# Low parts of weights by adding DMAs, sums of squares on TensorE, and shared copies in the first mixer of a two-block transformer

## The chip, the cores and the metric

The kernel runs as one program on one core of a Trainium2 chip. The core has five engines that each run their own list of instructions in order and meet by semaphores: PE (TensorE, matrix products), DVE (VectorE), ACT (ScalarE), POOL (GpSimd) and SP (SyncE, which here only issues DMAs). PSUM holds the results of TensorE; everything else that an engine works on lies in SBUF. The metric is the device time of one execution in microseconds. Before the change the median of 3 runs is 2953.4 us (2951.94 to 2958.28).

## The reference

Two transformer blocks on 256 positions of width 2048, in float32. The change lies in the mixer of the first block:

```python
hn = _rmsnorm(h, attn_norm_w[l])
proj = hn @ w_in[l]                         # 2048 x 1856
u, c_q, c_kv, k_pe = jnp.split(proj, split_at, axis=-1)
y_ssm = _s5_group(u, ...)                   # 64 groups, 64 states, scan over 256 positions,
                                            # gelu, times sigmoid(y @ w_glu + b_glu)
y_mla = _mla_group(c_q, c_kv, k_pe, ...)    # norm, up projections, rotation, 8 causal heads
y = jnp.concatenate([_rmsnorm(y_ssm, ssm_out_norm_w[l]),
                     _rmsnorm(y_mla, mla_out_norm_w[l])], axis=-1)
h = h + y @ w_out[l]
h = h + _conv_ffn(_rmsnorm(h, ffn_norm_w[l]), ...)
```

The second block (a chunked state-space mixer and an RWKV-7 mixer, then a gated feed-forward part) and the first block's feed-forward part are computed by code that does not change.

## The kernel before

**Weights in two parts.** Float32 products are made on TensorE from numbers of reduced precision (type fp32r). A weight block of eight 128 x 128 tiles is a *piece* (`piece`, L322 to L336): SP loads it into `raw` (128 x 1024, 512 KB, 4 buffers), ACT rounds it into the high part `wh` (L329, 3 buffers), and the low part `wl` = raw − wh (L335, 3 buffers) is made by DVE or POOL. A counter chooses: every piece adds `self.pl` to `self.pc`, and when that reaches 1 the piece goes to POOL. `self.pl` is taken from the table `PB`, stage by stage: 0.625 gives POOL five pieces of eight, 1.0 all of them, 0.0 none. The activations are split the same way (`split`, L407 and L408). In the first mixer (`self.one` true) `mm` then issues three matmuls per tile, high weight by low activation, high by high, low by high (L349 to L351), 24 per piece, in this order tile by tile.

**The stages of the first mixer** (`block1_mix`), in the order of the program:

1. The input is loaded and split; the squares of its 16 tiles are summed for the norm (`Sums`), whose result `r1` scales the results of the first product when they leave PSUM (L381, into `u` or `c`).
2. The product with `w_in`, 15 column tiles of two pieces: tiles 0 to 2 with `PB[0]`, 3 to 7 with `PB[1]`, and 12, 13, 14, 8, 9, 10, 11 with `PB[2]`. Between them lie the four batches of the state-space layer (`ssm_batch`: expansions by `ssm_ef`, L616, L617 and L620, on DVE; small products, L359 and L659; evictions to `X` on ACT, L669), two scans over batches 0, 1 and 2, 3 (`ssm_scan`, L701 to L722, all on DVE), and the expansions of the output side (`ssm_f`, the same lines on POOL).
3. The small norms and projections of the attention (`small_norm`, `mla_proj`, ten pieces with `PB[3]`), the attention itself, and the activation of the state-space layer (`ssm_g`), which gathers its result by sixteen copies per batch on ACT (L755).
4. The product with `w_out`: 16 pieces of the attention half, 8 pieces of the `w_glu` product between them (`glu_tile`), then 16 pieces of the state-space half; `PB[4]` and `PB[5]`.

**Sums of squares.** `Sums` squares each tile on ACT (L209), POOL adds the squares up (L213), and TensorE sums the running total and the last square over partitions, with a column of ones (`mmc`, L359, two matmuls of 64 columns each time).

**What sets the order.** A scheduler orders every engine's list when the program is built, by dependences and its estimates; the order of the source is its starting point, not its result. A piece's copy has to wait until the matmuls of three pieces earlier have let go of their buffer. SP loads ahead as far as the four `raw` buffers allow; a `raw` buffer comes free when its low part is made.

**Other helpers.** `rope_tables` (L473 to L477 with its callees) makes sine and cosine of the rotation, from a DMA of the positions; `bcast` and `rsqrt` (L419 to L434) turn a sum into a scale for all partitions, by way of POOL and TensorE.

Of the kernel before, what the change touches and what calls it, by code (L numbers as in the profile page):

```python
# [10 lines left out]
F32 = mybir.dt.float32  # L11
F32R = mybir.dt.float32r
I32 = mybir.dt.int32
AF = mybir.ActivationFunctionType
ALU = mybir.AluOpType
# [3 lines left out]
P = 128  # L19
# [169 lines left out]


X0 = [(0, 2, 0, 4), (2, 2, 4, 4), (4, 4, 8, 8), (8, 4, 0, 0), (12, 4, 0, 0)]
PB = [0.0, 0.625, 1.0, 1.0, 0.625, 0.625]
EV = [(1, 2), (1, 4, 5, 8), 4, 1]
TK = [18, 17, (44, 19), (34, 12), 6, 10, 56, 7, (7, 7, 7), 14, 16]

# [1 line left out]
class Sums:  # L197


    def __init__(self, k, n, c=0, tag="qa", out=None, last=True):  # L200
        self.k, self.n, self.c, self.i, self.out, self.last = k, n, c, 0, out, last
        self.acc = k.t(tag=tag)

    def add(self, src, scale=1.0, on_act=True):
        k, nc = self.k, self.k.nc
        self.i += 1
        sq = self.acc if self.i == 1 else k.t(tag="sq")
        if on_act:
            nc.scalar.activation(sq, src, AF.Square, scale=scale)  # L209
        else:  # L210
            nc.vector.tensor_tensor(sq, src, src, op=ALU.mult)
        if 1 < self.i < self.n:
            nc.gpsimd.tensor_tensor(self.acc, self.acc, sq, op=ALU.add)  # L213
        if self.i == self.n:
            first = self.out is None
            self.out = k.ssq_start() if first else self.out
            for q in (self.acc, sq):
                for b in range(2):
                    c = self.c + b
                    k.mmc(self.out[:, c:c + 1], q[:, b * P:b * P + P], k.ones[:, 0:1],  # L220
                          first and b == 0 and q is self.acc, self.last and b == 1 and q is sq)


class K:
    def __init__(self, ctx, tc, A, dbg=None):
        self.tc, self.nc, self.A, self.ctx = tc, tc.nc, A, ctx
        self.dbg = dbg or {}
        E = ctx.enter_context
        self.cst = E(tc.tile_pool(name="cst", bufs=1))
        self.raw = E(tc.tile_pool(name="raw", bufs=4))  # L230
        self.wh = E(tc.tile_pool(name="wh", bufs=3))
        self.wl = E(tc.tile_pool(name="wl", bufs=3))
        self.tmp = E(tc.tile_pool(name="tmp", bufs=3))
        self.sm = E(tc.tile_pool(name="sm", bufs=2))
        self.big = E(tc.tile_pool(name="big", bufs=1))
        dr = E(tc.tile_pool(name="dr", bufs=1, space=bass.MemoryType.DRAM))
        self.nd = [dr.tile([32, 32, 32], F32, name=f"n_d{i}") for i in range(8)]
        self.nd2 = [dr.tile([32, 32, 32], F32, name=f"m_d{i}") for i in range(8)]
        self.csd = dr.tile([32, T], F32, name="cs_d")
        self.ysd, self.yrd, self.hd, self.hd2 = [dr.tile([P, 16, T], F32, name=n)  # L240
                                                 for n in ("ys_d", "yr_d", "h_d", "i_d")]
        self.pn = E(tc.tile_pool(name="pn", bufs=1, space=PSUM))
        self.pp = E(tc.tile_pool(name="pp", bufs=1, space=PSUM))
        self.banks = list(range(7))
        self.bgs = []
        self.fibs = []
        self._n = 0
        self.pc = 0
        self.pl = 0
        self.hp = 400  # L250
        self.one = False

    def nm(self, s="t"):
# [69 lines left out]
    def piece(self, ap, nb):  # L323
        nc = self.nc
        r = self.raw.tile([P, KP * P], F32, name=self.nm("raw"), tag="raw")[:, :nb * P]
        h = self.wh.tile([P, KP * P], F32R, name=self.nm("wh"), tag="wh")[:, :nb * P]
        l = self.wl.tile([P, KP * P], F32R, name=self.nm("wl"), tag="wl")[:, :nb * P]
        nc.sync.dma_start(r, ap)
        nc.scalar.activation(h, r, AF.Copy)  # L329
        self.pc += self.pl  # L330
        eng = nc.vector
        if self.pc >= 1:
            eng = nc.gpsimd
            self.pc -= 1
        eng.tensor_tensor(l, r, h.bitcast(F32), op=ALU.subtract)  # L335
        return h, l  # L336

# [402 lines left out]
    def ssm_g(self, b):  # L740

        nc = self.nc
        V, S = nc.vector, nc.scalar
        Z = self.Z[b]
        g = self.ph.tile([P, 8, 64], F32, name=self.nm("sg"), tag="sg", bufs=1)
        S.activation(g, Z, AF.Square)
        V.tensor_scalar(g, g, 0.044715, 1.0, ALU.mult, ALU.add)
        V.tensor_tensor(g, g, Z, op=ALU.mult)
        S.activation(g, g, AF.Tanh, scale=math.sqrt(2.0 / math.pi))
        V.scalar_tensor_tensor(g, g, 1.0, Z, ALU.add, ALU.mult)  # L750
        for q in range(4):
            for s in range(4):
                dst = self.u[32 * q:32 * q + 32, 2 * b:2 * b + 2].rearrange("p j (c s) -> p j s c", s=4)[:, :, s]
                sl = slice(32 * s, 32 * s + 32)
                S.activation(dst, g[sl, 2 * q:2 * q + 2], AF.Copy)  # L755
        for j in range(2 * b, 2 * b + 2):
            self.split(self.gl[:, j], self.u[:, j])

# [34 lines left out]
    def small_norm(self, x, nt, dst, gname):  # L793

        nc = self.nc
        q = Sums(self, nt)
        for i in range(nt):
            q.add(x[:, i])
        r = self.rsqrt(q.out, nt * P)
        rb = self.t(tag="ev")  # L800
        self.bcast(r, rb)
        for i in range(nt):
            y = self.t(tag="ev")
            nc.vector.tensor_tensor(y, x[:, i], rb, op=ALU.mult)
            self.split(dst[:, i], y, self.v(gname, i))
# [92 lines left out]

    def block1_mix(self):
        nc, A = self.nc, self.A  # L900
        self.one = True
        xx = self.xx_new()
        self.hh = [self.b([8, T], f"hh{i}") for i in range(2)]
        pc0 = []
        for k, kn, w0, wn in X0:
# [3 lines left out]
            for i in range(k, k + kn):  # L909
                last = self.split(xx(i), self.h(i), self.v("attn_norm_w", i))  # L910
        self.setup2()
        pst = Sums(self, 16)
        with self.tc.issue_after(last.ins):
            for k in range(16):
                pst.add(self.h(k))
# [2 lines left out]
        self.ssm_pre()  # L918
        self.bglu = self.ssm.tile([P, 8], F32, name="bglu")
        nc.vector.tensor_scalar(self.bglu, self.vs("ssm_b_glu"), 0.5, None, ALU.mult)  # L920
        self.rope_tables()
        self.kpe = [self.mla.tile([P, T], F32, name=f"kpe{i}") for i in range(2)]
        for i in range(2):
            nc.vector.memset(self.kpe[i], 0.0)
# [3 lines left out]
        for n in range(8):  # L928
            self.pl = PB[0] if n < 3 else PB[1]
            p = self.gemm(A["w_in"][n], 16, xx, pcs=pc0 if n == 0 else None)  # L930
# [5 lines left out]
        c = self.ssm.tile([P, 8, T], F32, name="c", tag="u")  # L936
        self.pl = PB[2]
        for i, n in enumerate((12, 13, 14, 8, 9, 10, 11)):
# [7 lines left out]
                    self.ssm_f(k)  # L946
            if i == 2:
                self.ssm_scan(2, 2)
            if i in (3, 4):
                self.ssm_y(i - 3)  # L950
            if i == 5:
# [45 lines left out]
        pst = Sums(self, 16)  # L997
        for n in range(16):
# [5 lines left out]
            nc.vector.tensor_tensor(self.h(n), self.h(n), t, op=ALU.add)  # L1004
            self.split(xx(n), self.h(n), self.v("ffn_norm_w", n))
            pst.add(self.h(n))
        self.one = False
        if "h1" in self.dbg:
            for i in range(2):
                nc.gpsimd.dma_start(self.dbg["h1"][:, 8 * i:8 * i + 8], self.hh[i])  # L1010
# [828 lines left out]
```

## Time and profile before

| | |
|---|---|
| median of 3 runs | 2953.4 us (2951.94 to 2958.28) |
| profiled execution | 2956.56 us, of which the span from first to last instruction is 2954.8 us |
| busy in the span: PE, DVE, ACT, POOL | 2808.0 us (95%), 1974.3 (67%), 1523.8 (52%), 889.5 (30%) |
| mean DMA rate | 166 GB/s |
| first mixer | from 0 to about 450 us |

Times in the profile are microseconds from the start of the span unless marked ns. An instruction is named by its line, its engine, its operation and its tiles, `out<-in`, with the buffers' numbers left out. A window's row has the stretch, its length, then for PE, PEld (the loading of weights into TensorE), DVE, ACT and POOL the busy time and in brackets the count of instructions; then the clock granted to TensorE as a part of full speed, the share of time in which the 16 DMA engines were busy, and the GB/s that they moved. A wait's row has the instruction that waited, the one it waited for, and then the microseconds in all, the number of times, and the longest. A row of a group has the count, the busy time, the mean duration, and the idle time of the engine just before.

### The profile page before, as it was taken

The numbers are of one execution on the slowest core, as the hardware profiler recorded it, in microseconds if no ns is written. First come the engines' busy times: TensorE is split into PE (matmuls) and PEld (weight loads), VectorE is DVE, ScalarE is ACT, GpSimd is POOL, SyncE is SP. The second block draws the span as 40 slices with busy tenths as digits, with TensorE's granted clock in tenths as the row PEclk, the third lists the DMA queues.
The fourth block names the chain that finished last, engine by engine and source line by source line (L and its number), as shares of the span: only waits on it lengthen the run. The fifth ranks groups of instructions, "written<-read, shape, count | busy, mean of one in ns | idle before, by whom it ended". The sixth has DMA issues, their size and how long they took to land.

```text
span 2954.8 us, 54809 instructions
## 1 busy us (share of the span) xinstructions
PE 2808.0 (95%) x21648; PEld 2530.9 (86%) x21648; DVE 1974.3 (67%) x3385; ACT 1523.8 (52%) x2569; POOL 889.5 (30%) x716
## 2 busy tenths in 40 slices
PE   6767899999999999999999999998999999999998
PEld 6766898888888888999998999988988888888887
DVE  9995578886378876887767767774674544354544
ACT  6527655555455555555545555553554444444454
POOL 6565573333333334100110111000023333333333
PEclk8887999999999999999999999999999999999999
DMA  4222255556655556555554444445755656655564
GB/s 165 82 81 78 88 175 180 183 190 181 187 188 187 186 181 199 196 184 185 183 165 127 134 124 132 125 144 152 249 183 185 191 181 186 189 189 185 187 183 151
DMA packets 178978, 490.37 MB, mean 166 GB/s; under 512 B 44416, under 2 KB 61600, under 8 KB 178208
## 3 DMA queue, kind: packets, MB, share of 16 engines
q1 hardware_dynamic: 176992, 483.13, 52.1%
q8 instruction: 170, 2.79, 0.4%
q0 software_dynamic: 288, 2.10, 0.2%
q10 hardware_dynamic: 1440, 1.63, 0.2%
q14 instruction: 88, 0.72, 0.1%
HBM read 474.17 MB, written 12.62 MB: 165 GB/s over the span
## 4 chain that ended last, share of the span: by engine, by line
PE 78%; DMA 2%; DVE 2%; ACT 1%; SPq 1%; issue 1%; POOL 0%; POOLq 0%; DVEq 0%; ACTq 0%
PE acc L353 35%; PE acc L354 18%; PE acc L349 7%; PE acc L350 6%; PE acc L351 6%; PE pc L1351 1%; PE pm L1468 1%; DVE wl L335 1%; PE pm L1630 1%; PE pc L1356 1%; PE py L1259 0%; DMA n_d<-hh 0%; PE pm L1351 0%; SPq L1532 0%; ACT wh L329 0%
## 5 line engine op out<-in xcount | busy, mean ns | idle before, releaser
L329 ACT ACTIVATE wh<-raw 128x1024 fp32r<-128x1024 f32 (+2 forms) x873 | 908.3, 1042 | 999.5 <-PE acc L353 459.8
L335 DVE TENSOR_TENSOR wl<-raw,wh 128x1024 fp32r<-128x1024 f32 (+2 forms) x682 | 861.1, 1263 | 602.7 <-ACT wh L329 595.8
L353 PE MATMUL acc<-xx,wh 128*128 128x512 f32 x2176 | 770.9, 396 | 0.5 <-ACT wh L329 0.5
L354 PE MATMUL acc<-xx,wl 128*128 128x256 f32 x2176 | 614.7, 283 | 0.8 <-DVE wl L335 0.8
L335 POOL TENSOR_TENSOR wl<-raw,wh 128x1024 fp32r<-128x1024 f32 (+1 forms) x191 | 454.6, 2381 | 532.4 <-ACT wh L329 517.0
L353 PEld LDWEIGHTS acc<-xx,wh 128*128 128x128 f32 x2176 | 409.9, 188 | 99.1 <-ACT wh L329 0.7
L354 PEld LDWEIGHTS acc<-xx,wl 128*128 128x128 f32 x2176 | 409.7, 188 | 1.5 <-DVE wl L335 1.4
L353 PE MATMUL acc<-B,wh 128*128 128x512 f32 x960 | 344.7, 396 | 0.0
L353 PE MATMUL acc<-X,wh 128*128 128x512 f32 x960 | 344.4, 396 | 0.0
L349 PE MATMUL acc<-B,wh 128*128 128x256 f32 x960 | 287.5, 300 | 5.6 <-ACT xx L379 3.2
L350 PE MATMUL acc<-B,wh 128*128 128x256 f32 x960 | 272.5, 284 | 0.0
L351 PE MATMUL acc<-B,wl 128*128 128x256 f32 x960 | 272.2, 284 | 0.0
L354 PE MATMUL acc<-B,wl 128*128 128x256 f32 x960 | 271.2, 282 | 1.0 <-POOL wl L335 1.0
L354 PE MATMUL acc<-X,wl 128*128 128x256 f32 x960 | 270.8, 282 | 0.0
L349 PE MATMUL acc<-X,wh 128*128 128x256 f32 x832 | 251.2, 302 | 5.8 <-ACT wh L329 4.5
L351 PE MATMUL acc<-X,wl 128*128 128x256 f32 x832 | 235.5, 283 | 0.8 <-DVE wl L335 0.8
L350 PE MATMUL acc<-X,wh 128*128 128x256 f32 x832 | 235.1, 283 | 0.0
L353 PEld LDWEIGHTS acc<-X,wh 128*128 128x128 f32 x960 | 180.5, 188 | 43.6
L353 PEld LDWEIGHTS acc<-B,wh 128*128 128x128 f32 x960 | 180.5, 188 | 43.4
L213 POOL TENSOR_TENSOR qa<-qa,sq 128x256 f32<-128x256 f32 x86 | 90.0, 1046 | 346.5 <-ACT sq L209 250.1
L349 PEld LDWEIGHTS acc<-B,wh 128*128 128x128 f32 x960 | 184.2, 192 | 11.3 <-ACT xx L379 3.4
L350 PEld LDWEIGHTS acc<-B,wh 128*128 128x128 f32 x960 | 184.3, 192 | 0.6
(497 smaller groups left out, 5255.9 us busy)
## 6 DMA issues: line engine op xcount, KB each, us to landing
raw<-in_w_up_dram SPq DMA_DIRECT2D x264, 512.0 KB, 3.6
raw<-in_w_in_dram SPq DMA_DIRECT2D x213, 512.0 KB, 3.6
raw<-in_w_down_dram SPq DMA_DIRECT2D x128, 448.0 KB, 3.9
raw<-in_w_out_dram SPq DMA_DIRECT2D x96, 512.0 KB, 4.3
raw<-in_w_gate_dram SPq DMA_DIRECT2D x88, 512.0 KB, 4.2
raw<-in_w_down_dram SPq DMA_DIRECT2D x64, 512.0 KB, 4.1
raw<-in_w_glu_dram SPq DMA_DIRECT2D x8, 512.0 KB, 3.5
cb<-cs_d SPq DMA_DIRECT2D x16, 256.0 KB, 3.9
```

The costliest lines, as they stand in the source:

```text
L213: nc.gpsimd.tensor_tensor(self.acc, self.acc, sq, op=ALU.add)
L329: nc.scalar.activation(h, r, AF.Copy)
L335: eng.tensor_tensor(l, r, h.bitcast(F32), op=ALU.subtract)
L349: nc.tensor.matmul(p[:, :T], h, x[:, 1], start=first, stop=False)
L350: nc.tensor.matmul(p[:, :T], h, x[:, 0], start=False, stop=False)
L351: nc.tensor.matmul(p[:, :T], l, x[:, 0], start=False, stop=last)
L353: nc.tensor.matmul(p, h, x.rearrange("p a b -> p (a b)"), start=first, stop=False)
L354: nc.tensor.matmul(p[:, T:], l, x[:, 0], start=False, stop=last)
L1351: self.nc.tensor.matmul(out[hs], lhsT[hs], rhs[hs], start=start, stop=stop)
L1356: self.nc.tensor.matmul(out[64 * h:64 * h + 64], lhsT(h), rhs(h), start=start, stop=stop)
L1468: nc.tensor.matmul(p[:, P * c:P * c + P], z[:, c], AR[:, c].rearrange("p a t -> p (a t)"), start=True, stop=True)
L1630: nc.tensor.matmul(pg[:, T * i:T * i + T], lw[:, 256 * i + P * k:256 * i + P * k + P], self.tgd[:, k], start=k == 0, stop=k == 1)
```

## The change

1. `PB[3]` becomes 0.0: the ten pieces of `mla_proj` give their low parts to DVE.
2. A flag `self.acc` is true in all of `block1_mix`. Where the counter says POOL and the flag is set, the low part is made in another way: a second ACT instruction writes raw times −1 into `wl`, rounded like `wh`, and POOL issues a DMA that adds `raw` to what stands there (`accum_op=ALU.add`). This meets 6 pieces of tiles 3 to 7, 14 of the later tiles, and 25 of the 40 pieces of stage 4.
3. `Sums` gets a way `pe=True`: TensorE adds up every square itself, four matmuls a square, and POOL adds nothing. It is used in the first norm and in `small_norm`.
4. The call of `rope_tables` moves behind the second scan.
5. `ssm_g` gives every second of its copies to DVE: 8 of 16 per batch, 32 in all.

```diff
-PB = [0.0, 0.625, 1.0, 1.0, 0.625, 0.625]
+PB = [0.0, 0.625, 1.0, 0.0, 0.625, 0.625]
...
-    def __init__(self, k, n, c=0, tag="qa", out=None, last=True):
-        self.k, self.n, self.c, self.i, self.out, self.last = k, n, c, 0, out, last
-        self.acc = k.t(tag=tag)
+    def __init__(self, k, n, c=0, tag="qa", out=None, last=True, pe=False):
+        self.k, self.n, self.c, self.i, self.out, self.last, self.pe = k, n, c, 0, out, last, pe
+        self.acc = None if pe else k.t(tag=tag)
...
+        if self.pe:
+            if self.i == 1:
+                self.out = k.ssq_start()
+            for b in range(2):
+                k.mmc(self.out[:, b:b + 1], sq[:, b * P:b * P + P], k.ones[:, 0:1],
+                      self.i == 1 and b == 0, self.i == self.n and b == 1)
+            return
...
         if self.pc >= 1:
+            self.pc -= 1
+            if self.acc:
+                nc.scalar.activation(l, r, AF.Copy, scale=-1.0)
+                nc.gpsimd.dma_start(l.bitcast(F32), r, accum_op=ALU.add)
+                return h, l
             eng = nc.gpsimd
-            self.pc -= 1
...
-                S.activation(dst, g[sl, 2 * q:2 * q + 2], AF.Copy)
+                if s % 2:
+                    V.tensor_copy(dst, g[sl, 2 * q:2 * q + 2])
+                else:
+                    S.activation(dst, g[sl, 2 * q:2 * q + 2], AF.Copy)
...
-        q = Sums(self, nt)
+        q = Sums(self, nt, pe=True)
...
-        self.one = True
+        self.one = self.acc = True
...
-        pst = Sums(self, 16)
+        pst = Sums(self, 16, pe=True)
...
-        self.rope_tables()
...
                 self.ssm_scan(2, 2)
+                self.rope_tables()
...
-        self.one = False
+        self.one = self.acc = False
```

The new lines stand at 335 to 348 in the changed file: L337 is the copy, L343 the negation, L344 the DMA and L347 the subtraction.

How the built lists change. First POOL in tiles 12 to 11, beside the two scans. `wl` is a low part; `ef`, `FA` and `FB` are the expansions of `ssm_f`; `rb` is a product of the rotation. Before:

```order
L616 TENSOR_TENSOR ef_2213<-PA,scq_2210 128x256
L335 TENSOR_TENSOR wl_1378<-raw_1376,wh_1377 128x1024
L335 TENSOR_TENSOR wl_1512<-raw_1510,wh_1511 128x1024
L617 TENSOR_TENSOR ef_2214<-PA,scq_2210 128x256
L335 TENSOR_TENSOR wl_1542<-raw_1540,wh_1541 128x1024
L335 TENSOR_TENSOR wl_1823<-raw_1821,wh_1822 128x1024
L335 TENSOR_TENSOR wl_1853<-raw_1851,wh_1852 128x1024
```

After:

```order
L344 DMA wl_1276<-raw_1274 128x1024
L344 DMA wl_1402<-raw_1400 128x1024
L344 DMA wl_1537<-raw_1535 128x1024
L344 DMA wl_1568<-raw_1566 128x1024
L344 DMA wl_1850<-raw_1848 128x1024
L344 DMA wl_1881<-raw_1879 128x1024
L344 DMA wl_1969<-raw_1967 128x1024
```

The subtractions are gone from the list and DMA issues stand in their places; the expansions that stood among them stand ahead of or behind this run.

Second DVE, at the tables of the rotation, before the first tile of `w_in`. `ev` holds the angle and what becomes of it, `k` and `xc` belong to the preparation of the state-space layer. Before:

```order
L778 TENSOR_SCALAR ev_460<-ev_460,vec 128x256
L506 SCALAR_TENSOR_TENSOR xc_252<-xc_252,xb_251 128x32
L473 TENSOR_SCALAR ev_465<-ev_460 128x256
L509 SCALAR_TENSOR_TENSOR k_249<-xc_252,xi_267 128x32
L474 TENSOR_SCALAR ev_465<-ev_465 128x256
```

After:

```order
L793 TENSOR_SCALAR ev_2164<-ev_2164,vec 128x256
L518 SCALAR_TENSOR_TENSOR xc_294<-xc_294,xb_293 128x32
L485 TENSOR_SCALAR ev_2169<-ev_2164 128x256
L521 SCALAR_TENSOR_TENSOR k_291<-xc_294,xi_309 128x32
L486 TENSOR_SCALAR ev_2169<-ev_2169 128x256
```

The numbers of the buffers show that the call was made later; the instructions stand in the same rows of the list, between the same neighbours.

Third ACT, in stage 4, among the tiles of `w_glu` (`ys` and `sq` are the split and the square of such a tile, `acc` is a PSUM tile). Before:

```order
L329 ACTIVATE wh_3816<-raw_3815 128x1024
L329 ACTIVATE wh_3857<-raw_3856 128x1024
L379 ACTIVATE ev_3770<-acc_3739 128x256
L765 ACTIVATE ev_3770<-ev_3770,bglu 128x256
L407 ACTIVATE ys_3408<-ev_3773,vec 128x256
L209 ACTIVATE sq_3777<-ev_3773 128x256
```

After:

```order
L337 ACTIVATE wh_3967<-raw_3966 128x1024
L343 ACTIVATE wl_3968<-raw_3966 128x1024
L337 ACTIVATE wh_4009<-raw_4008 128x1024
L391 ACTIVATE ev_3920<-acc_3889 128x256
L337 ACTIVATE wh_4043<-raw_4042 128x1024
L343 ACTIVATE wl_4044<-raw_4042 128x1024
L780 ACTIVATE ev_3920<-ev_3920,bglu 128x256
```

A negation (L343) follows the copy of each piece whose low part is made by a DMA, and the evictions and activations stand behind it.

Last DVE, at the end of the second scan (L731 to L734), where `mla_proj`'s low parts now appear:

```order
L731 TENSOR_TENSOR sc_2156<-AK,X_497 128x196
L347 TENSOR_TENSOR wl_2698<-raw_2696,wh_2697 128x1024
L732 TENSOR_TENSOR sc_2157<-AK,X_497 128x196
L733 TENSOR_TENSOR X_497<-X_497,sc_2156 128x4x7x7
L819 TENSOR_TENSOR ev_2522<-c,ev_2517 128x256
L819 TENSOR_TENSOR ev_2526<-c,ev_2517 128x256
L734 TENSOR_TENSOR X_497<-X_497,sc_2157 128x4x7x7
```

In the list before the change no low part stands among these rows (L719 to L722 there).

## Rows read from the trace of the kernel before

**Rows 1.** Windows, by stage: engines' busy us (instructions), granted clock, DMA share, GB/s.

```profile
0.00:36.00 36.00, 22.41 (x146) 20.74 (x147) 31.24 (x86) 24.77 (x50) 23.90 (x31) 0.91 0.70 242
36.00:123.00 87.00, 69.31 (x837) 65.58 (x835) 80.50 (x159) 48.97 (x99) 51.30 (x44) 0.86 0.31 98
123.00:164.00 41.00, 30.20 (x386) 28.94 (x386) 40.12 (x92) 21.99 (x40) 12.66 (x5) 0.88 0.20 65
164.00:228.00 64.00, 35.63 (x301) 32.53 (x301) 63.14 (x106) 11.15 (x17) 40.04 (x29) 0.72 0.23 77
228.00:332.00 104.00, 77.68 (x530) 69.29 (x529) 49.52 (x96) 75.94 (x185) 49.08 (x44) 0.82 0.16 51
332.00:450.00 118.00, 112.94 (x941) 110.80 (x941) 85.99 (x95) 62.55 (x102) 87.20 (x61) 0.99 0.53 174
```

**Rows 2.** Waits of DVE, 36 to 228 us: total us, times, longest.

```profile
DVE B L620 <- PE sp L659: 3.8, 2, 2.8
```

**Rows 3.** Waits of PE, 36 to 228 us, the two longest.

```profile
PE sp L359 <- ACT X L669: 8.9, 1, 8.9
PE sp L359 <- DVE B L620: 8.8, 4, 3.2
```

**Rows 4.** Timeline of DVE, 133 to 141 us: start us, us, instruction.

```profile
133.20 0.65 DVE L704 TENSOR_TENSOR X<-X,sc 128x256 f32<-128x256 f32 x1
133.88 2.60 DVE L701 TENSOR_TENSOR sc<-A,X 128x256 f32<-128x256 f32 x1
136.40 2.87 DVE L702 TENSOR_TENSOR sc<-A,X 128x256 f32<-128x256 f32 x1
```

**Rows 5.** Timeline of POOL, 133 to 141 us.

```profile
133.40 5.32 POOL L335 TENSOR_TENSOR wl<-raw,wh 128x1024 fp32r<-128x1024 f32 x2 [15.30 <-ACT wh L329]
```

**Rows 6.** Groups by line of POOL, 36 to 226 us.

```profile
L335 POOL TENSOR_TENSOR wl<-raw,wh 128x1024 fp32r<-128x1024 f32 x23 | 59.5, 2590 | 56.9 <-ACT wh L329 47.7 <-issue 8.8 <-PE sp L359 0.3
...
L213 POOL TENSOR_TENSOR qa<-qa,sq 128x256 f32<-128x256 f32 x2 | 1.6, 780 | 0.0
```

**Rows 7.** Groups by line of DVE, 228 to 332 us.

```profile
L335 DVE TENSOR_TENSOR wl<-raw,wh 128x1024 fp32r<-128x1024 f32 x2 | 2.5, 1226 | 6.8 <-ACT wh L329 6.8
```

**Rows 8.** Groups by line of ACT, 228 to 332 us.

```profile
L755 ACT ACTIVATE u<-sg 32x128 f32<-32x128 f32 x64 | 27.3, 427 | 1.2 <-DVE sg L750 0.5
```

**Rows 9.** Timeline of ACT, 236 to 252 us.

```profile
241.38 6.97 ACT L755 ACTIVATE u<-sg 32x128 f32<-32x128 f32 x16
```

**Rows 10.** Waits of PE, 228 to 332 us, the longest.

```profile
PE acc L829 <- ACT xx L832: 7.7, 1, 7.7
```

**Rows 11.** Groups by line of DVE, whole program: copies of 32 elements.

```profile
L583 DVE COPY A<-AK 128x32 f32<-128x32 f32 x2 | 0.4, 182 | 0.0
```

**Rows 12.** Waits of PE, 332 to 450 us, all of them.

```profile
PE acc L349 <- DVE ev L381: 6.4, 4, 2.4
```

**Rows 13.** Groups by line of POOL, 332 to 450 us.

```profile
L335 POOL TENSOR_TENSOR wl<-raw,wh 128x1024 fp32r<-128x1024 f32 x24 | 58.1, 2421 | 6.9 <-ACT wh L329 5.8
```

**Rows 14.** Timeline of PE, 339 to 349 us.

```profile
340.04 0.28 PE L349 MATMUL acc<-X,wh 128*128 128x256 f32 x1
...
342.87 0.28 PE L349 MATMUL acc<-B,wh 128*128 128x256 f32 x1
```

**Rows 15.** Groups by line of ACT, 332 to 450 us.

```profile
L329 ACT ACTIVATE wh<-raw 128x1024 fp32r<-128x1024 f32 x38 | 40.0, 1052 | 24.2 <-PE acc L350 17.9 <-issue 3.0 <-POOL hh L990 1.8
```

**Rows 16.** DMA issues of the page: KB each, median us to landing.

```profile
raw<-in_w_in_dram SPq DMA_DIRECT2D x213, 512.0 KB, 3.6
...
raw<-in_w_out_dram SPq DMA_DIRECT2D x96, 512.0 KB, 4.3
```

**Rows 17.** Line 1699, transfers of 1024 KB that POOL issues.

```profile
L1699 POOL DMA_DIRECT2D h_d<-hh x2: 571/672/772, 1139.1 to 1201.0; - x2
...
DMA to landing us min/median/max: 5.5/5.9/6.3
```

**Rows 18.** DMA, 332 to 450 us.

```profile
DMA packets 5605, 20.55 MB, mean 174 GB/s; under 512 B 612, under 2 KB 612, under 8 KB 5596
```

More of the change, by code (lines that the diff above doesn't have):

```diff
@@ L206, in add @@
         self.i += 1
-        sq = self.acc if self.i == 1 else k.t(tag="sq")
+        sq = self.acc if self.i == 1 and not self.pe else k.t(tag="sq")
         if on_act:
@@ L250, in __init__ @@
         self.hp = 400
+        self.acc = False
         self.one = False
```

## The prediction

> **What bounds the kernel now.** I read four views in this order: the windows by stage, the waits of VectorE and TensorE inside the stages, the two timelines of one stretch, and the groups by line. The windows [rows 1] show that the first mixer ends near 450 us and has three regimes. From 36 to 228 us VectorE is busy 80.5 + 40.1 + 63.1 = 183.8 of 192 us, and TensorE only 69.3 + 30.2 + 35.6 = 135.1. VectorE hardly waits: 3.8 us for a PSUM tile is its longest entry [rows 2]. TensorE waits for what the serial state-space work gives it, 8.9 and 8.8 us at the top [rows 3]. So here the end is set by how long VectorE's own instructions take. From 228 to 332 us nobody is full; TensorE has 77.7 and ScalarE 75.9 of 104 us, and they wait for each other. From 332 to 450 us TensorE is busy 112.9 of 118 us, and its only wait is 6.4 us for VectorE's evictions, none for a weight piece [rows 12]. Behind 450 us nothing is changed.
>
> One thing does not show in the waits. Two subtractions on GpSimd start at 133.40 us and take 5.32 us [rows 5]; the two VectorE instructions beside them take 2.60 and 2.87 us, where the same shape just before took 0.65 [rows 4]. VectorE loses (2.60 − 0.65) + (2.87 − 0.65) = 4.17 us to two subtractions, 2.1 us each. It counts as busy while it stands still.
>
> **The change, part by part.** Sums are made against the profiled execution, 2956.6 us (span 2954.8 and 1.8 around it); the median of the runs shown, 2953.4, is 3.2 lower, and I subtract 3.2 at the end.
>
> *Low parts, 36 to 228 us.* GpSimd makes 23 subtractions there, 59.5 us [rows 6]. Twenty become a ScalarE negation and an adding DMA (6 of tiles 3 to 7, 14 of tiles 8 to 14); the other three belong to the first projection pieces and go to VectorE. If every one costs VectorE what the two in [rows 4] did, 23 × 2.1 = 48 us of standing still go. The bound below is zero: the rows show the coincidence in one place, and the group can hide elsewhere. The three pieces cost VectorE 3 × 1.23 = 3.7 us [rows 7]; the order places one of them before the second scan's last instruction and two right behind it. ScalarE gets 20 × 1.05 = 21 us [rows 15], where it was busy 49.0 + 22.0 + 11.2 = 82 of 192 us, so that is covered by its idle time, unless a negation that waits for a buffer holds up the Z copies and evictions queued behind it. GpSimd is left with the state-space expansions, which now start earlier. What is late next is TensorE: with 48 − 4 = 44 us gone, 148 us hold its 135 us, so only 13 us of its waits may remain out of what are tens now, and the chain of small instructions behind the 8.9 us wait for X [rows 3] does not get shorter. I take −36, about four fifths; both ends −48 and 0, and the likely ones −44 and −15.
>
> *The adding DMAs in that stretch.* A piece is now two ScalarE passes, 2.1 us, and a landing; the 7 tiles after 123 us take (228 − 123) / 14 = 7.5 us a piece with three buffers, so even a 10 us landing is covered there, and the DMA engines are busy 0.20 to 0.31. I cost it at nothing. Without that cover it is the price worked out below for the later stretch.
>
> *Sums of squares by TensorE.* The first norm's sixteen additions on GpSimd become 64 one-column matmuls instead of 8, beside 22.4 us of TensorE work in 36 [rows 1]; the small norms' additions, 1.6 us in two [rows 6], go the same way. The scale r1 is first needed at the first tile's eviction, and VectorE is busy 31.2 of 36 us before it. Bounds −3 and +3, taken as 0.
>
> *Rotation tables.* The call stands later in the source, but VectorE's row order is the same at the place where it was. 0; the bound above, if the tables displaced something, is 1 us.
>
> *Copies and projections, 228 to 332 us.* Sixty-four copies on ScalarE take 27.3 us, 427 ns each [rows 8]; half go to VectorE: 32 × 0.43 = 13.7 us off ScalarE, 32 × about 0.2 = 6.4 us on VectorE (0.18 us is the nearest copy, of fewer columns and more partitions [rows 11]; ends 0.18 and 0.43). What this is worth is read from the one long wait: TensorE stands 7.7 us for a ScalarE eviction [rows 10] that is queued behind sixteen of these copies, 6.97 us from 241.38 [rows 9]. With eight it stands some 3.5 us less, and the later three batches can give as much together, −7. Against that VectorE takes seven more projection pieces (7 × 1.23 = 8.6 us) at 49.5 + 6.4 + 8.6 = 64.5 of 104 us; it isn't full, but each piece can stand in front of a softmax step. I put 3 us for that. −7 + 3 = −4, ends −15 and +8.
>
> *Low parts, 332 to 450 us.* Here 25 of 40 pieces change. TensorE eats a piece in 342.87 − 340.04 = 2.83 us [rows 14]. A low-part buffer is one of three, so a new piece must be made within 2 × 2.83 = 5.66 us of its buffer's release. GpSimd does so now: 1.05 us copy and 2.42 us subtraction [rows 13, 15], 3.5 us. After the change the chain c is copy 1.05, negation 1.05, some 0.2 for the issue (the queue's own 0.57 to 0.77 us of issuing, [rows 17], overlaps other pieces), and the landing L: c = 2.3 + L. Twenty-five of forty is five in eight. The slowest path steps from one adding piece to the next on the same buffer, three pieces on; five such steps and one piece of TensorE cover 16 pieces: 5(2.83 + c) + 2.83 against 16 × 2.83 = 45.3, so 16 pieces lose 5c − 28.3 and 40 lose 2.5 times that. Before, no DMA adds, so L has bounds: a 512 KB weight load lands in 3.6 us, in 4.3 for w_out [rows 16]; a 1024 KB transfer issued by GpSimd in 5.5 to 6.3 [rows 17]. An add reads two operands and writes one, so it lies between: I take the middle of 3.6 and 6.3, rounded, 4.9. Then c = 7.2 and the loss 2.5 × 7.7 = 19 us. At 3.6 it is 2.5 × 1.2 = 3; at 5.9 it is 2.5 × 12.7 = 32.
>
> ScalarE's 25 × 1.05 = 26 us more make 63 + 26 = 89 of 118 us, not full. The GpSimd subtractions that lengthen VectorE here don't set the end, since TensorE does not wait for VectorE beyond those 6.4 us.
>
> The GpSimd row, 5.5 to 6.3 us for 1024 KB, is the only one on a software queue [rows 17]. The Trainium skill ("DMA: Bandwidth & Descriptors", section "Anatomy of one DMA — SWDGE (gpsimd) path") fits such a transfer by 2.0 us and the bytes at 436 GB/s, an estimate of 4.4 us for 1024 KB, which this trace doesn't bear out, and 3.2 for 512 KB. By that rule c = 5.5, the last loss would be 0, and the whole −40.
>
> Sum: −36 − 4 + 19 = −21. 2956.6 − 21 = 2935.6 profiled, 2932 as a median.
>
> **Rivals.**
>
> *Short landing.* The adds land like the weight loads, 3.6 us, and the early stretch gives 44: −44 − 4 + 3 = −45, 2908. For it: small transfers, from and to on-chip memory. Against: two reads, and the GpSimd row.
>
> *The adds crowd the transfers of the last stretch (the slower side).* 20.55 MB moved there [rows 18] at a DMA share of 0.53 [rows 1]. Twenty-five adds of 0.52 MB are 13.1 MB: counted once the share becomes 0.53 × 33.7 / 20.55 = 0.87, counted twice, for two reads, 1.21. At 1.21 the stretch can't last less than 118 × 1.21 = 143 us, and landings grow with the queue. At L = 8 us c = 10.3 and the loss is 2.5 × 23.2 = 58: −36 − 4 + 58 = +18, 2971. It decides from where the loss equals the gain of 40: 5c − 28.3 = 16, c = 8.9, L = 6.6, just above the longest 1024 KB landing. Against it: 0.7 of the engines' time is already reached in the first 36 us without any loss that I can see.
>
> The skill's page "Collectives: The Full Stack", section "The bandwidth ceiling: the fold count and why AG ≠ RS ≠ AR", says that an add inside the DMA engine moves half as much per second because it needs two source reads; no trace here has such an add. By that rule the count is 1.21, a loss of 25 us, and the sum −36 − 4 + 25 = −15.
>
> *VectorE's gain is handed on.* The long instructions shrink, but TensorE's clock (0.72 to 0.88 granted, [rows 1]) and the state-space chain take over, and negations stand in front of evictions: −15 − 4 + 19 = 0, 2953. For it: TensorE's 135 us in a stretch that would have 148. Against: its waits are for VectorE's results as much as for ScalarE's, and they move up with them.
>
> **How the numbers follow.** Forecast 0.45, short landing 0.22, crowded transfers 0.20, gain handed on 0.13. The forecast's own range is 2915 to 2950. The range with the rivals reaches from a little below the short landing, 2902, to the crowded case, 2972. About 0.2%, 5.9 us, is what a measurement of this kernel can tell from no change: faster is under 2947.5, slower over 2959.3. The forecast and the short landing are nearly all faster, 0.65, with 0.03 from the rest; the handed-on case gives most of the 0.12 for no change; slower is 0.20.
>
> **What would show it.** Right: the VectorE instructions of the scans at 0.65 us throughout; the second scan's end some 36 us earlier than the 228 where that stage ends now; the landing of line 344's DMA between 4 and 6 us; TensorE from there to the end of the mixer with waits for low parts of some 19 us; the stretch of the projections about as long as before. Wrong: long VectorE instructions without GpSimd subtractions beside them (then the theory of the standing still falls); a landing over 6.6 us; TensorE's waits in the first two hundred microseconds for ScalarE instead of VectorE.

## The result and the profile after

The changed kernel takes 2917.0 us (median of 4 runs, 2915.0 to 2919.5) against 2955.8 in the same comparison (4 runs): a ratio of 0.9867, 95% interval 0.9855 to 0.9878, 38.8 us faster. The forecast was 2932 with a range of 2902 to 2972; 21 us were expected. The profiled execution took 2916.5 us (span 2914.7), 40.1 less than the one before.

Where the time went, by points of the program that both kernels have (us from the start of the span):

| | before | after | gained so far |
|---|---|---|---|
| last tile of `w_in` leaves PSUM (last `c`) | 223.2 | 190.7 | 32.5 |
| second scan ends | 226.5 | 190.7 | 35.8 |
| first softmax instruction | 286.1 | 235.5 | 50.6 |
| first eviction of `w_out` | 332.3 | 274.5 | 57.8 |
| last eviction of `w_out` ends | 448.7 | 414.7 | 34.0 |
| end of the span | 2954.8 | 2914.7 | 40.1 |

So the stretch of the scans gave 36 us as forecast, the stretch of the projections and the attention 22 instead of 4, and the product with `w_out` took back 24. The windows of the changed kernel, cut at these points, the last one 1 us behind (columns as in [rows 1]):

```profile
36.00:190.70 154.70, 124.92 (x1492) 118.33 (x1492) 139.99 (x312) 98.04 (x174) 68.95 (x86) 0.88 0.66 164
190.70:274.50 83.80, 71.26 (x558) 63.74 (x558) 57.57 (x142) 66.67 (x159) 18.53 (x23) 0.92 0.30 88
274.50:415.80 141.30, 118.22 (x940) 114.36 (x940) 56.78 (x96) 82.25 (x123) 51.49 (x61) 0.96 0.88 228
```

VectorE is still nearly full to the end of the scans (140.0 of 154.7 us). In the last row the share of the DMA engines has risen from 0.53 [rows 1] to 0.88, and TensorE is busy 118 of 141 us where it was busy 113 of 118. Its waits there, of the changed kernel:

```profile
PE acc L363 <- DMA wl<-raw: 22.3, 12, 3.1
PE acc L361 <- DVE ev L393: 4.3, 1, 4.3
PE acc L361 <- ACT wh L337: 0.2, 1, 0.2
```

The first row has no counterpart in [rows 12]: twelve times TensorE stands for an adding DMA. That DMA (line 344), from 275 to 416 us: issue time in ns min/median/max, and landing in us.

```profile
L344 POOL DMA_DIRECT2D wl<-raw x22: 851/876/899, 274.5 to 403.9; - x22
...
DMA to landing us min/median/max: 4.6/5.7/8.4
```

5.7 us, where 4.9 were estimated from [rows 16, 17]. And the DMA queues from 275 to 416 us (packets, MB, share of the 16 engines' time):

```profile
q0 software_dynamic: 3312, 12.06, 46.5%
q1 hardware_dynamic: 5472, 19.93, 41.1%
```

The adds are 12.06 MB of 31.99 but take more of the engines' time than all weight loads. Over 141 us that is 65.6 us for 23 adds of 0.524 MB, 2.85 us each, against 58.0 us for 38 loads, 1.53 each: 1.87 times as much.

What VectorE gained can be seen on the groups that both kernels have (count, busy us, mean ns). Before, 0 to 260 us:

```profile
L620 DVE TENSOR_TENSOR B<-ef,ef 64x256 f32<-64x256 f32 x32 | 23.4, 732 | 4.2 <-PE sp L659 3.8
L702 DVE TENSOR_TENSOR sc<-A,X 128x256 f32<-128x256 f32 x14 | 16.0, 1142 | 0.0
```

After (L632 and L714 are the same lines):

```profile
L632 DVE TENSOR_TENSOR B<-ef,ef 64x256 f32<-64x256 f32 x32 | 16.8, 525 | 4.1 <-PE sp L671 3.5
L714 DVE TENSOR_TENSOR sc<-A,X 128x256 f32<-128x256 f32 x14 | 10.8, 770 | 0.0
```

The same work, 32 and 14 instructions, takes 27.6 us instead of 39.4. Over all 240 instructions of the expansions and the two scans it is 121.1 us instead of 156.9, 35.8 less.

### The profile page after: what moved, and what is told of

It reads as the page before. It is cut to its first block, busy times and chain, and to the rows that moved or that the text cites. A ratio compares the mean times of both kernels' runs of the same rounds, so it can differ in the third digit from the quotient of the medians.

```text
span 2914.7 us, 55170 instructions
## 1 busy us (share of the span) xinstructions
PE 2796.9 (96%) x21776; PEld 2519.0 (86%) x21776; DVE 1906.5 (65%) x3427; ACT 1550.6 (53%) x2582; POOL 770.4 (26%) x690
## 4 chain that ended last, share of the span: by engine, by line
PE 84%; DVE 5%; DMA 4%; ACT 3%; issue 2%; SPq 1%; POOL 0%; POOLq 0%; DVEq 0%; ACTq 0%
PE acc L365 36%; PE acc L366 18%; PE acc L361 8%; PE acc L363 7%; PE acc L362 7%; DMA wl<-raw 2%; PE pc L1366 1%; PE pm L1483 1%; DVE wl L347 1%; ACT wh L337 1%; PE pc L1371 1%; PE pm L1645 1%; PE py L1274 0%; PE pn L371 0%; PE pm L1366 0%
## 5 line engine op out<-in xcount | busy, mean ns | idle before, releaser
L337 ACT ACTIVATE wh<-raw 128x1024 fp32r<-128x1024 f32 (+2 forms) x873 | 908.9, 1042 | 1026.3 <-PE acc L365 464.8
L347 DVE TENSOR_TENSOR wl<-raw,wh 128x1024 fp32r<-128x1024 f32 (+2 forms) x692 | 868.4, 1256 | 604.4 <-ACT wh L337 600.2
L347 POOL TENSOR_TENSOR wl<-raw,wh 128x1024 fp32r<-128x1024 f32 (+1 forms) x136 | 318.0, 2338 | 450.5 <-ACT wh L337 450.5
L363 PEld LDWEIGHTS acc<-B,wl 128*128 128x128 f32 x960 | 182.4, 190 | 7.0 <-DMA wl<-raw 7.0
```

Source lines behind the costliest of these rows:

```text
L363: nc.tensor.matmul(p[:, :T], l, x[:, 0], start=False, stop=last)
```

## The experiments

Ratios are to the kernel before, in the same comparison, with 95% intervals.

**The w_out stretch without adds.** In the changed kernel:

```diff
         self.pl = PB[4]
+        self.acc = False
```

> The changed kernel, with the low parts of the last stretch (the 40 pieces of w_out and w_glu) made on GpSimd by subtraction again, as before the change; all else as changed. Theory (the rotation of three low-part buffers, 5(2.83 + c) per 16 pieces): the 22.3 us in which TensorE waits for adding DMAs after 290 us go away, the stretch from the first to the last eviction of w_out falls from 140 us to the 116 us it took before, and the time from 2917 to about 2894 us. Rival (the stretch is longer because the transfers of the earlier stages, now closer together, leave weight loads late): the time stays within 5 us of 2917 and TensorE waits for raw or wh instead.

2900.6 us, 0.9812 (0.9798 to 0.9826): 16.5 below the changed kernel's median. First to last eviction takes 277.5 to 392.2, 114.7 us instead of 140.2, and TensorE's only wait there is

```profile
PE acc L361 <- DVE ev L393: 6.7, 4, 2.4
```

So the adds cost that stretch 25 us. Which of the two reasons costs them, the rotation or the crowding, this run doesn't tell.

**The parts alone.** Each is put into the kernel before by itself. First the adds, in `w_in` only:

```diff
+            if self.acc:                      # in piece(), as in the change
+                nc.scalar.activation(l, r, AF.Copy, scale=-1.0)
+                nc.gpsimd.dma_start(l.bitcast(F32), r, accum_op=ALU.add)
+                return h, l
...
         self.pl = PB[3]
+        self.acc = False
```

> The kernel before, with one part of the change alone: the 20 low parts of tiles 3 to 14 of w_in by negation and adding DMA. Theory (VectorE stands still beside GpSimd's subtractions): the second scan ends 32 to 36 us earlier than 226.5, the time is about 2920 us; if the unforecast 22 us of the projection stage came from GpSimd's state-space work being done earlier, they come along and the time is about 2900. Rival (sums on TensorE and the earlier first scale are what moved the scans): the second scan ends less than 15 us earlier, 2940 us or more.

2924.2 us, 0.9891 (0.9877 to 0.9906), 31.9 faster. The second scan ends at 196.3, 30.2 earlier, and from there to the first eviction of `w_out` it takes as long as before (106.0 and 105.8): the other 22 us don't come from here. Then the projections:

```diff
-PB = [0.0, 0.625, 1.0, 1.0, 0.625, 0.625]
+PB = [0.0, 0.625, 1.0, 0.0, 0.625, 0.625]
```

> The kernel before, with one part alone: the ten projection pieces' low parts on VectorE instead of GpSimd. If the unforecast 22 us of the projection stage come from here (no subtraction beside the norms, the splits and the softmax), the time falls by 10 to 20 us to about 2940; three subtractions fewer in the scans give up to 6 us of it. By the prediction's own term it costs 3 us there and gains at most the 6: about 2952.

2942.9 us, 0.9955 (0.9942 to 0.9969), 13.2 faster. And the copies:

```diff
-                S.activation(dst, g[sl, 2 * q:2 * q + 2], AF.Copy)
+                if s % 2:
+                    V.tensor_copy(dst, g[sl, 2 * q:2 * q + 2])
+                else:
+                    S.activation(dst, g[sl, 2 * q:2 * q + 2], AF.Copy)
```

> The kernel before, with one part alone: half of the 64 copies on VectorE. By the prediction's term, 7 us less: about 2949. If the 22 us of the projection stage come mainly from ScalarE's queue (7.7 us wait behind sixteen copies, and the softmax behind three more batches), 12 to 20 us less: about 2940. If other waits end last there, no change within 3 us.

2945.8 us, 0.9961 (0.9948 to 0.9975), 10.3 faster. The three make 55.4, and the first experiment, which has all three and the sums, gained 55.5. In the projections' run the second scan ends 12 us *later* than before and the first softmax comes 13.7 *earlier*. The ten projection pieces follow each other faster. GpSimd before, four of its last five:

```profile
250.67 2.36 POOL L335 TENSOR_TENSOR wl<-raw,wh 128x1024 fp32r<-128x1024 f32 x1 [5.07 <-issue]
...
255.60 2.39 POOL L335 TENSOR_TENSOR wl<-raw,wh 128x1024 fp32r<-128x1024 f32 x1 [0.73 <-ACT wh L329]
...
260.90 2.38 POOL L335 TENSOR_TENSOR wl<-raw,wh 128x1024 fp32r<-128x1024 f32 x1
...
270.86 2.40 POOL L335 TENSOR_TENSOR wl<-raw,wh 128x1024 fp32r<-128x1024 f32 x1 [1.31 <-ACT wh L329]
```

VectorE in the experiment, four of its last six:

```profile
244.75 1.23 DVE L335 TENSOR_TENSOR wl<-raw,wh 128x1024 fp32r<-128x1024 f32 x1 [4.35 <-ACT wh L329]
247.81 1.23 DVE L335 TENSOR_TENSOR wl<-raw,wh 128x1024 fp32r<-128x1024 f32 x1
249.73 1.22 DVE L335 TENSOR_TENSOR wl<-raw,wh 128x1024 fp32r<-128x1024 f32 x1 [0.69 <-ACT wh L329]
...
263.90 1.21 DVE L335 TENSOR_TENSOR wl<-raw,wh 128x1024 fp32r<-128x1024 f32 x1
```

A piece is made in half the time, and the last is ready at 265 instead of 273. But it is not GpSimd that holds the pieces up. Four of its last five pieces start within 0.13 us of the end of ScalarE's rounding into `wh`, and TensorE waits for no low part there. Its waits from 226.5 to 286 us before:

```profile
PE acc L829 <- ACT xx L832: 7.7, 1, 7.7
PE pm L786 <- ACT ev L379: 3.6, 1, 3.6
PE acc L349 <- ACT xx L379: 3.2, 1, 3.2
PE pm L786 <- DVE ra L788: 0.5, 1, 0.5
```

The longest three in the experiment, from 226 to 272.5 us:

```profile
PE acc L349 <- ACT ev L379: 2.8, 1, 2.8
PE acc L349 <- DVE B L408: 2.3, 1, 2.3
PE acc L829 <- ACT xx L379: 2.2, 1, 2.2
```

The waits for ScalarE's evictions fall from 14.5 to 5.0 us, though ScalarE has the same work. Two things about its list differ. Before, three of the batches of sixteen copies (at 241.38, 258.59 and 274.18) stand ahead of the last evictions that the first softmax needs, in the experiment two. And the first batch starts at 235.75 instead of 241.38: ahead of it ScalarE waits for VectorE's four instructions of a small norm (L804), which take 4.53 us before, beside a subtraction on GpSimd, and 2.50 in the experiment. How much of the 13 us each gives is not shown; no run separates them.

**The w_in pieces on VectorE, without adds.** In the kernel before:

```diff
-PB = [0.0, 0.625, 1.0, 1.0, 0.625, 0.625]
+PB = [0.0, 0.0, 0.0, 1.0, 0.625, 0.625]
```

> The kernel before, with the 20 low parts of tiles 3 to 14 of w_in made by VectorE itself, without any adding DMA or negation. Theory (each GpSimd subtraction makes VectorE stand still for about 2.1 us, and VectorE's time sets the scans): 20 x 1.25 us are added to VectorE and 20 x 2.1 us of standing still go, so the second scan ends about 17 us earlier than 226.5 although VectorE does more, the scan instructions of 128x256 take 0.65 us throughout, and the time is about 2939 us. Rival (the gain of the adding DMAs is that the work leaves GpSimd's own list, or VectorE's long instructions have another cause): VectorE only gets 25 us more, the second scan ends 15 us or more later, 2970 us or more.

2918.1 us, 0.9872 (0.9856 to 0.9889), 38.2 faster, with neither of the two outcomes that I wrote down. The 240 instructions take 131.4 us instead of 156.9, so the standing still is real and was taken away; but the second scan ends at 241, 15 us later than before, as the rival said, and the time is nevertheless not worse than with the adds alone. VectorE in this run:

```profile
192.04 0.42 DVE L381 TENSOR_TENSOR c<-acc,R 128x256 f32<-128x256 f32 x1
...
240.81 0.35 DVE L722 TENSOR_TENSOR X<-X,sc 128x196 f32<-128x196 f32 x1
...
253.94 0.55 DVE L862 SCALAR_TENSOR_TENSOR as<-pm,cstt 128x384 f32<-128x384 f32 x1
```

The first row is the last tile of `w_in` leaving PSUM, at 192 as in the changed kernel; the second is the scan's last instruction; the third the first softmax, 13 us behind it. The softmax follows the last `c` by 62 us here, 63 before, 61 with the adds alone. In the changed kernel it is 45, with the projections alone 51. It does not follow the scan's end. The end of the mixer hangs on the last `c`, which stands in VectorE's list between the scan's instructions.

This edit does one thing more, and so do the five below that set other numbers for `PB[1]`, `PB[4]` or `PB[5]`. The counter `self.pc` is not set back when the mixer ends. In both kernels and in the other runs it leaves the mixer at 0.25; in these six it leaves at 0, 0.5 or 0.75, so that behind the mixer other pieces go to GpSimd. From the last eviction of `w_out` to the end of the span these six take 2490.1 to 2500.3 us, the other eight kernels 2500.0 to 2514.9. No run changes the counter alone. But the 6 us between this run and the adds alone arise behind the mixer: the last eviction of `w_out` comes at nearly the same time, first with the adds alone, then here:

```profile
416.85 0.41 DVE L386 TENSOR_TENSOR ev<-acc,R 128x256 f32<-128x256 f32 x1
```

```profile
417.57 0.41 DVE L381 TENSOR_TENSOR ev<-acc,R 128x256 f32<-128x256 f32 x1
```

**Four buffers for low parts.** In the changed kernel:

```diff
-        self.wl = E(tc.tile_pool(name="wl", bufs=3))
+        self.wl = E(tc.tile_pool(name="wl", bufs=4))
-    BUFS = {"lo256": 2, "ev256": 6, "sq256": 2, ... "th256": 2,
+    BUFS = {"lo256": 1, "ev256": 5, "sq256": 1, ... "th256": 1,
```

> The changed kernel with four buffers for low parts instead of three; to make room, one buffer each less for four small temporaries (lo, th, sq, ev), which act mostly outside the stretch that is read. Theory (the loss of the w_out stretch is the rotation of three buffers against a chain of 2.3 + 5.7 = 8.0 us): with four the chain has 3 x 2.83 = 8.5 us, TensorE's 22.3 us of waits for adding DMAs there fall below 6, the stretch from the first to the last eviction from 140 to about 120 us. Rival (the adds crowd the weight loads on the DMA engines, busy 0.88 there): waits for adding DMAs or for raw and wh stay above 15 us, whatever the buffers; a landing grows over 7 us.

2927.8 us, 0.9902 (0.9887 to 0.9917). The buffers that were taken away cost it time elsewhere (the first tile of `w_in` leaves PSUM at 60.4 instead of 41.4), so only the stretch is read: it takes 133.1 us (277.6 to 410.7). Its waits for adds and its landings:

```profile
PE acc L363 <- DMA wl<-raw: 19.0, 10, 4.1
```

```profile
DMA to landing us min/median/max: 4.6/7.2/10.1
```

The rotation theory asked for under 6 us and 120; the rival's 15 us and its longer landings came. With another buffer more adds are under way at once, and each takes longer. The DMA engines' busy time is the same, 0.93 x 133.1 = 124 and 0.88 x 140.2 = 123 us.

**Half the adds.** In the changed kernel:

```diff
-PB = [0.0, 0.625, 1.0, 0.0, 0.625, 0.625]
+PB = [0.0, 0.625, 1.0, 0.0, 0.3125, 0.3125]
```

> The changed kernel with 12 or 13 adding DMAs in the w_out stretch instead of 25, none of two pieces in a row, the other pieces' low parts on VectorE. If the DMA engines' time is what limits that stretch (123 us of busy time with the adds, 62 without, so 2.5 us an add), 62 + 31 = 93 of some 116 us leave room: landings fall to about 5 us, the stretch to 120 us or less, and the time to about 2900. If a chain longer than the rotation of three buffers is what costs (c = 2.3 + 4.9 = 7.2 against 5.66, 1.5 us for each add whose neighbours don't wait), about 19 us of loss remain, the stretch is 133 us or more, and TensorE waits over 15 us for adds.

2890.5 us, 0.9769 (0.9756 to 0.9782): 26.5 us below the changed kernel. The stretch takes 117.1 us (275.3 to 392.4), 23 less:

```profile
275.30:392.40 117.10, 111.17 (x927) 108.15 (x928) 71.10 (x105) 71.25 (x111) 46.36 (x49) 1.00 0.77 216
```

```profile
PE acc L363 <- DMA wl<-raw: 1.8, 4, 0.8
```

```profile
DMA to landing us min/median/max: 4.5/5.0/6.2
```

At c = 2.3 + 5.0 = 7.3 each add is still 1.6 us longer than the rotation allows, yet only 1.8 us are lost over all of them. So it is not the rotation that costs; the crowding fits this run and the one before. Half the adds are also half the negations on ScalarE, and no run takes away one without the other; but TensorE waited only 0.2 us for ScalarE in this stretch with all of them. At the last eviction of `w_out` this kernel is 22.3 us ahead of the changed one; the rest of the 26.5 comes behind the mixer.

**Sums of squares, and combinations.** The first experiment's kernel with the sums on GpSimd again:

```diff
-        pst = Sums(self, 16, pe=True)
+        pst = Sums(self, 16)
...
-        q = Sums(self, nt, pe=True)
+        q = Sums(self, nt)
```

> The changed kernel with GpSimd subtractions in the w_out stretch (the first experiment), and with the sums of squares of the first norm and of the small norms on GpSimd again. The three parts tried alone gave 31.9, 13.2 and 10.3 us, 55.4 in all, as much as the first experiment's 55.5; by that the sums give nothing and the time stays at 2901 within 4 us. Rival (the sums bring the first scale earlier, the parts only happen to add up): 2906 us or more.

2896.0 us, 0.9794 (0.9780 to 0.9809), 4.6 below the first experiment: neither value I expected. The last eviction of `w_out` comes 4.8 earlier, at 387.4, the earliest of all. The first experiment's kernel with more adds in `w_in` (`PB[1]` = 1.0):

> The first experiment's kernel with all pieces of tiles 3 to 7 by adding DMA, not five of eight: four pieces of 1.25 us less on VectorE, which is busy nearly all of the time there. By VectorE as the bound: 5 us less, about 2896. Rival (TensorE already waits 10 us for adds in this stretch and ScalarE gets four negations more): no change within 3 us, or up to 5 us more.

2889.2 us, 0.9769 (0.9754 to 0.9785), 11.4 below the first experiment. But the mixer's profile shows no gain (last eviction of `w_out` at 394.0 against 392.2); the 13.7 us between the two profiled executions come up behind it, where the counter's other fraction gives GpSimd other pieces. So VectorE's 5 us did not reach the end of the mixer. Both together:

> The two best changes so far together: all pieces of tiles 3 to 14 by adding DMA (2889.2) and the sums of squares on GpSimd (4.6 us less than on TensorE), GpSimd subtractions in the w_out stretch. If they add up, 2885 us; if both only bring the same eviction of the last tile earlier, 2889.

2901.1 us, 0.9801 (0.9788 to 0.9814). They don't add up; the sum of squares, 4.6 us better on GpSimd in one pair, is 11.9 us worse in the other (4.9 at the last eviction of `w_out`). And without any add (`PB` = 0, 0, 0, 0, 0.625, 0.625, sums on GpSimd):

> No adding DMA anywhere: the changed kernel with the low parts of all of w_in and of the projections on VectorE, GpSimd subtractions in the w_out stretch, and the sums of squares on GpSimd; of the change only the shared copies and the projections on VectorE are left. If the parts add up (38.2 for w_in on VectorE, 13.2 for the projections, 10.3 for the copies, 61.7 in all), 2895 us, as good as with adds in w_in. If VectorE, which then has 30 pieces more than before in the first 240 us, is the bound there, the gains overlap and the time is 2905 or more.

2908.4 us, 0.9831 (0.9817 to 0.9844). The gains overlap: the last `c` comes at 189.6 and the first softmax at 239.9, against 191.7 and 239.5 in the first experiment, but the second scan ends at 252.5 instead of 191.7. VectorE does it beside the softmax, and the first eviction of `w_out` comes at 291.4, 14 us later than there. Last, more adds in `w_in` and half of them in `w_out` (`PB` = 0, 1.0, 1.0, 0, 0.3125, 0.3125):

> The changed kernel with one row of numbers changed: all pieces of tiles 3 to 7 by adding DMA instead of five of eight (11.4 us faster in one comparison), and 12 or 13 adds in the w_out stretch instead of 25 (2890). If both hold, 2880 us; if the extra adds in w_in only crowd what the stretch won, or the first gain was one of order alone (it didn't add to the sums on GpSimd), 2890 again.

2899.9 us, 0.9806 (0.9788 to 0.9824). It is no better than its parts. The best are the two at 0.9769, of which the kernel with half the adds has most of its gain where it was looked for.

The move of the rotation tables was not run: with the call put back, the lists of all five engines are the same, row by row.

## Why the prediction was right and where it was not

The time lies in the range, on the right side, at nearly twice the forecast gain (39 for 21). One term is off by 18 us; that 2917 still lies in the forecast's own range, 2915 to 2950, is the width of the range and in part luck.

*Low parts up to the scan's end: −36 forecast, −35.8 measured, with the right price for the standing still and a deduction that came from elsewhere.* VectorE does stand still beside GpSimd's subtractions, and the pair of [rows 4, 5] is not an extreme one. Two more long instructions of VectorE, and the two subtractions beside them, in the kernel before:

```profile
167.06 2.77 DVE L702 TENSOR_TENSOR sc<-A,X 128x256 f32<-128x256 f32 x1
169.75 2.83 DVE L703 TENSOR_TENSOR X<-X,sc 128x256 f32<-128x256 f32 x1
```

```profile
166.62 5.44 POOL L335 TENSOR_TENSOR wl<-raw,wh 128x1024 fp32r<-128x1024 f32 x2
```

Of the 240 instructions before, 43 have a subtraction beside them, 22 subtractions in all. They take 47.7 us longer than the same instructions (by their medians) with no computation of GpSimd beside them, 2.2 us a subtraction; in the three other runs that keep eight or more it is 2.1 to 2.3. The forecast took 2.1 and 48. All of it goes in the changed kernel. What comes back is something the forecast left out: GpSimd's other work, above all its expansions, holds VectorE up too, 12.4 us before and 21.4 after, and the instructions with nothing beside them take some 3 us more. An expansion beside a scan in the changed kernel:

```profile
153.73 1.66 DVE L714 TENSOR_TENSOR sc<-A,X 128x256 f32<-128x256 f32 x1
```

```profile
153.80 2.20 POOL L632 TENSOR_TENSOR FA<-ef,ef 64x256 f32<-64x256 f32 x2
```

So the scans are not at 0.65 us throughout, as the prediction asked, and there are long instructions without a subtraction beside them, which it named as a sign against the theory. The theory holds in a wider form: none of the 240 with no computation of GpSimd beside it is over 0.80 us in either kernel. The forecast's deductions, 4 us for three pieces on VectorE and 8 for what TensorE would hold up, had other grounds; that they make up about as much is luck. What was also wrong is the point at which this stretch was measured: not the scan's end but the last `c` sets what follows, as the run with the pieces on VectorE shows. In the changed kernel both fall together, so the number came out.

*Adding DMAs in that stretch, at nothing: too low.* TensorE waits for them there too, in the changed kernel from 36 to 228 us:

```profile
PE acc L363 <- DMA wl<-raw: 10.0, 8, 3.4
```

What that costs is not shown: without adds the same twenty pieces gave 38.2 us instead of 31.9, but the end of the mixer came no earlier. The pace of 7.5 us a piece was a mean; pieces come in bursts. Four adds from 95.2 us on are issued within 12 us and land in 5.0, 6.0, 8.1 and 6.6 us.

*Copies and projections, −4 forecast, −22 measured: the step that failed.* The copies gave 10.3 for 7. The projections were booked as a cost of 3, for VectorE instructions in front of softmax steps; they gave 13.2. I had counted what VectorE gets and nothing else. The wait that the copies' term was read from, TensorE for ScalarE's evictions, moves with the projections too, from 14.5 to 5.0 us, and GpSimd's subtractions, which this stretch loses, held up VectorE here as they did in the scans. Which of these gives how much stays open.

*Adds in the w_out stretch, +19 forecast, +24 measured (25 against the kernel without them): the size near, the mechanism not.* The rotation by the measured landing, c = 8.0, would cost 2.5 x (40 − 28.3) = 29 us, near enough to be taken for a confirmation. Four buffers and half the adds show that it is not the rotation; what fits is the DMA engines' time: 62 us of it without adds, 123 with. This was the mechanism of the second rival, at the price that its count gave before the queue was added (25), not at its 58.

An add takes 1.87 times as much of the engines' time as a load. The Trainium skill ("Collectives: The Full Stack", section "The bandwidth ceiling: the fold count and why AG ≠ RS ≠ AR") says this of the reduce-scatter between cores: half as much per second as a plain gather, for two source reads. This trace agrees for an add within one core, and the loss that the rule gave, 25 us, is the measured one. The fit of the Trainium skill ("DMA: Bandwidth & Descriptors", section "Anatomy of one DMA — SWDGE (gpsimd) path") gives an estimate of 3.2 us for 512 KB, below the shortest add seen, 4.5 us.

*Sums and rotation tables, 0 each.* The parts alone leave nothing for the sums in the first experiment, but the two pairs with and without them differ by 4.6 and −11.9 us (4.8 and −4.9 at the last eviction of `w_out`). What they are worth stays open; it depends on what else is in the lists. The tables are 0.

*The rest.* Behind the mixer the profiled execution gains 6 us more, though nothing is changed there: the lead is 34.0 us at the last eviction of `w_out`, 37.0 at 500 us and 40.2 from 2060 us on. Others lose there: the kernel without adds in the w_out stretch is 22.5 us ahead of the changed one at that eviction and 11.8 at the end of the span. I can't settle this. With the counter's other fractions on top, it means that differences under some 10 us in a median can't be read as effects of an edit in the mixer; the time at which the mixer ends tells more.

## What to carry to other kernels

When work moves from one engine to another, look again at the longest wait of the stage and at every list that feeds it, not only at whom the work burdens: the projections' low parts were booked as a cost of 3 us and gave 13, and the waits that shrank were for ScalarE. Look for a counter that carries an edit past its stage. Before moving work to DMA, add up the engines' busy time of the densest stretch, with adds counted twice; where the sum passes the stretch's length, spread them thinner: with half as many adds the stretch was 23 us shorter. And look for the instruction that the next stage waits for, not the last one of the stage: the scans of two kernels here end at 192 and 252 us, and the attention begins at 239.5 and 239.9.

## What was not expected of the hardware

An adding DMA within SBUF, 128 x 1024 in float32, lands in 4.5 us at least. In the w_out stretches the medians are 5.0 us with the DMA engines busy 0.77 of the time, 5.7 at 0.88 and 7.2 at 0.93. The share alone doesn't set it: from 93 to 191 us of the changed kernel, where the adds come in bursts, the median is 6.2 at 0.73.

```profile
DMA to landing us min/median/max: 4.6/6.2/8.4
```

```profile
q0 software_dynamic: 2160, 7.87, 44.5%
q1 hardware_dynamic: 2992, 9.31, 28.1%
```

An add takes 2.9 us of the engines' time there too (43.6 us for 15), 1.87 times a load's. Its issue holds GpSimd for 0.88 us, so twenty-five of them are 22 us of its time. With 23 of them among 38 weight loads of 512 KB, the loads of `w_out` land in 5.1 us instead of 4.1.
